# Twelve tiles of v under the inverse of the small blocks, four in the scan, and the adaptive sums ordered behind the masks of the scan preparation

## The chip, the cores and the metric

The kernel runs on one core of a Trainium2 chip. The metric is the device time of one execution in microseconds (us). The engines are TensorE (PE, matrix products; its weight loads are listed apart as PEld), VectorE (DVE), ScalarE (ACT), GpSimd (POOL) and SyncE (SP, which issues most transfers).

## The reference, cut to what matters

The program is a trunk of two layers for one sequence of 256 tokens and 2048 channels, in float32. Layer 0 mixes tokens with an RWKV-7 time mix, layer 1 with a convolution module; each is followed by a gated channel mixer (FFN). Before each of the four sub-layers the input is normalised and modulated by shift, scale and gate vectors made from a conditioning vector c; these vectors are the matrix-vector products called adaptive sums here. What the change touches is the time mix of layer 0:

```python
mod = silu(c) @ ada_w[i] + ada_b[i]            # the adaptive sums: 6 vectors of 2048 a layer
sh_m, sc_m, g_m, sh_f, sc_f, g_f = split(mod, 6)
r, k, v = einsum('nbtc,ncd->nbtd', x_rkv, w_rkv)
def step(S, inp):                              # one token, a 64 x 64 state for each of 32 heads
    sa = einsum('bhij,bhj->bhi', S, a_t)
    S = S * w_t + sa[..., None] * b_t + v_t[..., None] * k_t
    return S, einsum('bhij,bhj->bhi', S, r_t)
y = group_norm(scan(step, S0, (r, decay, k, v, -kk, kk * a)))
out = ((y + bonus) * g) @ w_o
x = x + g_m * out
h = modulate(rms_norm(x), sh_f, sc_f);  x = x + g_f * conv_glu_ffn(h)
```

## The kernel before, in words

Channels lie on the 128 partitions in 16 tiles (KT), each with two heads; tokens lie along the free axis. Products whose weights are streamed from DRAM come in two kinds. A split product rounds the weight to a short-mantissa part `hi` (ScalarE, L232) and a rest `lo` (VectorE or GpSimd, L233) and runs three matmuls for each of 16 pieces (L243 to L245, 48 a tile). A native product (`linear_native`, L306) runs one fp32 matmul a piece on the raw weight and needs no other engine.

The scan is not done token by token. The 256 tokens are cut into four chunks of 64 (NC_ = 4), and within a chunk the dependence is a triangular system, whose inverse is built from blocks of 32. VectorE inverts all the small blocks at once (`inv_step`, L592 to L599, helper lines L151 and L157), in two halves; the result X goes to DRAM (dT and dTn, L642 and L646) and is read back in another layout for each channel tile (`prep_load2`, L676 and L677). While VectorE inverts, PE makes the first V0 = 8 of 16 tiles of v by `v_tile`, with native products.

Then comes the scan stage, L652 to L887. For each channel tile f there is

- `prep_gen`: products of keys and queries (L704, called twice), a transpose (L712) copied by ScalarE (L713), two masks on VectorE (L710 for `strict`; L716, `gr`, for `incl`, both recorded at helper line L157), the completion of the inverse (L724, L749, copied by VectorE at L752), the centred v (L740) and a bonus (L755);
- `chain_gen`: four dependent chunks, each with L769, a copy on ScalarE (L774), L782, a copy on ScalarE (L784), L788 and the state update on VectorE (L793 or helper L160 called from L791);
- `gn_gen`: the group normalisation, for tiles 0 to 3, 4 to 7, 8 to 11, 12 and 13, 14 and 15 together (L805 to L831);
- and, as filler between these, `v_gen` (the other eight tiles of v, as split products) and `wo_gen` (the first NWO tiles of the output projection, half of their rows).

A heap written by hand sets the order of PE in this stage: each generator yields a planned delay, `at(t, ...)` puts it in at a planner time, PD = 13 units are one channel tile's period, and PE takes its instructions in the order in which the heap emits them (`manual_schedule`). The v_gen of the i-th split tile starts at (V1 + i VP) PD, here 13 i. The other engines' instructions, and SP's transfers, are ordered by the framework's scheduler, which simulates the program and gives each engine the instruction that is ready first; the order is then fixed, and each engine works through its own in turn.

The adaptive sums of later pieces have no close user. `ada` loads 1 MB of weights (L206) and makes one vector piece on VectorE with two multiply-and-sum instructions of 1024 columns (L209; the profile prints CUSTOM_DVE_ANT_0, the order ISA; each is followed by a short read of the accumulator). `bg_gen` emits one sum at planner time 0 and then one each 10 units (BGT, L859; each 7 units, BGT2, from the sum BGN on). Sums without a release condition may be put by the scheduler anywhere on VectorE's order where their weights are there.

Of the kernel before, what the change touches and what calls it, by code (L numbers as in the profile page):

```python
# [14 lines left out]
ALU = mybir.AluOpType  # L15
# [3 lines left out]
P = 128  # L19
# [7 lines left out]
L = 64  # L27
NC_ = T // L
# [3 lines left out]
GN_EPS = 64e-5  # L32
NS = 44
NT = 26
V0 = 8
RP = 1
PL = 10
PUP = 1.05
# [10 lines left out]
BG_G = 2  # L49
BGT = 10.0  # L50
VS = 0.42
V1 = 0.0
VP = 1.0
KM = 10
TPE = (1,)*14+(3,14)
TPO = (2,)*14+(4,5)
# [56 lines left out]
def trunk_kernel(ctx: ExitStack, tc: tile.TileContext, a, out):  # L113
    nc = tc.nc
# [17 lines left out]
    def slot512():  # L132
        return slot().rearrange("p a t -> p (a t)")[:, :2 * T]
# [22 lines left out]
    def vmul(o, x, y):  # L156
        nc.vector.tensor_tensor(out=o, in0=x, in1=y, op=ALU.mult)  # L157

    def stt(o, x, s, y, op0=ALU.mult, op1=ALU.add):
        nc.vector.scalar_tensor_tensor(out=o, in0=x, scalar=s, in1=y, op0=op0, op1=op1)  # L160
# [11 lines left out]
    def K(n):  # L172
        o, w = COFF[n]
        return cst[:, o:o + w]
# [6 lines left out]
    incl = K("incl").rearrange("p (c t) -> p c t", c=2)  # L181
# [10 lines left out]
    def mod(l, piece, f):  # L192
        return md[l][:, piece * KT + f:piece * KT + f + 1]
# [7 lines left out]
    def ada(l, piece, f, r=None):  # L201
        parts = 4 if r else TQ if l == 0 and piece != 5 else 2
        w = C // parts
        if r is None:
            r = raw_tile()
            nc.sync.dma_start(out=r, in_=a["ada"][l, piece, f])  # L206
            r = [r[:, q * w:(q + 1) * w] for q in range(parts)]
        for q in range(parts):
            nc.vector.tensor_tensor_reduce(  # L209
                out=r[q], in0=r[q], in1=cb[:, q * w:(q + 1) * w], scale=1.0,  # L210
                scalar=mod(l, piece, f) if q else pc("ada_b", (l * 6 + piece) * KT + f),
                op0=ALU.mult, op1=ALU.add, accum_out=mod(l, piece, f))
        if piece in (1, 4):
            g = "gam_mix" if piece == 1 else "gam_ffn"
            j = 0 if piece == 1 else KT
            stt(geff[l][:, j + f:j + f + 1], mod(l, piece, f), 1.0, pc(g, l * KT + f), ALU.add, ALU.mult)
# [3 lines left out]
    def bg(n):  # L220
        for _ in range(min(n, len(jobs))):
            ada(*jobs.pop(0))
# [44 lines left out]
    def linear(src, ops, tag=None, cols=T, eng=None, step=1024):  # L267
        return linears([src], ops, tag, cols, eng, None, step)[0]
# [45 lines left out]
    def split_x(src, o):  # L314
        nc.scalar.copy(o[:, 0, :T], src)  # L315
        vsub(o[:, 1, :T], src, o[:, 0, :T])
# [207 lines left out]
    def r_more(n):  # L524
        for _ in range(n):
            if rnext[0] < KT:
                for q in range(RP):
                    r_load(rnext[0] + q)
                r_tile(rnext[0])
                rnext[0] += 1  # L530
# [55 lines left out]
    def v_tile(f):  # L586
        acc = linear_native(vraw.pop(f) if f in vraw else load_w(a["w_rkv"][2, f]), xv32, ("c", "y")[f % 2])
        vt[f] = t1()
        nc.scalar.copy(vt[f], acc[:, :T])
# [34 lines left out]
    for s in range(1, 31):  # L624
# [3 lines left out]
        if s % NF == 1:  # L628
            if rnext[0] < KT:
                r_more(1)  # L630
            elif len(vt) < V0:
                v_tile(len(vt))
    r_more(KT)
    xv = []
    for f in range(KT):
        xv.append(slot(F32R))
        split_x(xv32[f], xv[f])
    while len(vt) < V0:
        v_tile(len(vt))
# [17 lines left out]
    def v_gen(f):  # L657
        acc = ps("mm")
        r = load_w(a["w_rkv"][2, f])
        yield 0  # L660
        for k0 in range(0, KT, 8):
            hi, lo = split_w(r, k0, k0 + 8, 512, VE[0])
            for k in range(k0, k0 + 8):
                mm_pair(acc, hi, lo, k - k0, xv[k], k == 0, k == KT - 1)
                yield VS
        vt[f] = t1()
        nc.scalar.copy(vt[f], acc[:, :T])
# [18 lines left out]
    def prep_gen(f):  # L686
        ari, bk, tt, tn = ld.pop(f)
        v = vt.pop(f)
        gr = slot512().rearrange("p (c h t) -> p c h t", c=NC_, h=2)
# [7 lines left out]
        def bank(mm):  # L697
            pg = ps("g")
            for c in range(NC_):
                mm(pg[:, c * P:(c + 1) * P], bk[:, c].rearrange("p j t -> p (j t)"), c)  # L700
            return pg.rearrange("p (c h t) -> p c h t", c=NC_, h=2)

        def times(j):
            return bank(lambda o, b, c: nc.tensor.matmul(o, lhsT=b, rhs=ari[j][:, c].rearrange("p h t -> p (h t)"), start=True, stop=True, skip_group_check=True))  # L704

        pg = times(0)
# [5 lines left out]
        pg = bank(lambda o, b, c: nc.tensor.transpose(out=o, in_=b, identity=ident))  # L712
        nc.scalar.copy(tk, pg.rearrange("p c h t -> p c (h t)"))  # L713
        yield PU
        pg = times(1)
        vmul(gr, pg, incl.unsqueeze(1).to_broadcast([P, NC_, 2, L]))  # L716
        yield 2.4

        py = ps("g")
# [116 lines left out]
    def xview(f):  # L836
        return xs[f // 2][:, f % 2, :T]

    def x_load(f):
        if xs[f // 2] is None:  # L840
            xs[f // 2] = slot()
            nc.sync.dma_start(out=xs[f // 2][:, :, :T], in_=a["xT"][:, f - f % 2:f - f % 2 + 2, :])


    def wo_gen(m):
        x_load(m)
        r = load_w(a["w_o"][m][:, :C // 2])
        yield 0
        acc = ps("mm")
        hi, lo = split_w(r, 0, KT // 2, 512, VE[0])  # L850
        for k in range(KT // 2):
            mm_pair(acc, hi, lo, k, yo[k], k == 0, k == KT // 2 - 1)
            yield VS
        stt(xview(m), acc[:, :T], mod(0, 2, m), xview(m))

    def bg_gen(n):
        for i in range(n):
            bg(1)
            yield BGT if i < BGN else BGT2  # L859

    heap, seq = [], [0]
# [1 line left out]
    def at(t, g):  # L863
        heapq.heappush(heap, (t, seq[0], g))
        seq[0] += 1

    for f in range(KT):
        at((f - 1) * PD, load_gen(f))
        at(f * PD, prep_gen(f))
        at((f + 1) * PD + 0.3, ("chain", f))  # L870
    for i, f in enumerate(range(V0, KT)):
        at((V1 + i * VP) * PD, v_gen(f))
    for fs in ((0, 1, 2, 3), (4, 5, 6, 7), (8, 9, 10, 11), (12, 13), (14, 15)):
        at((fs[-1] + 3) * PD + 3.0, gn_gen(fs))
    jobs[:0] = [(0, 2, f) for f in range(NWO)]
    jobs += [(0, 2, f) for f in range(NWO, NG)]
    at(0, bg_gen(99))
    for m in range(NWO):
        at(WO0 * PD + m * WOP, wo_gen(m))
    with tc.manual_schedule(engines={mybir.EngineType.PE}):  # L880
# [229 lines left out]
    with tc.manual_schedule(engines=CME):  # L1110
        for f in range(KT):
            e0, e1 = (nc.gpsimd if i >= LOV else nc.vector for i in (2 * f, 2 * f + 1))
            pg = linear(a["w_pw1"][KT + f], ops, "g", T + 2, e0, LST)
# [11 lines left out]
        with tc.manual_schedule(engines=TME):  # L1125
# [30 lines left out]
            for f in range(max(KT + 4, AST + NAQ)):  # L1156
# [11 lines left out]
                if 0 <= g < KT:  # L1168
                    (nc.gpsimd if g % XP == XP - 1 else nc.vector).tensor_tensor(
                        out=cops[g][:, 1, :T], in0=tv[g], in1=cops[g][:, 0, :T], op=ALU.subtract)  # L1170
# [130 lines left out]
```

## Time and profile before

| what | value |
|---|---|
| time, median of 3 runs | 2644.01 us (2635.43 to 2644.99) |
| the profiled execution | 2645.53 us |
| its span, first to last instruction | 2643.8 us |
| granted TensorE clock, mean | 0.974 |
| PE, DVE, ACT, POOL busy | 94%, 77%, 51%, 19% |
| DMA over the span | 237 GB/s read and written |

The times come from runs without a profile; the trace and all its rows come from one execution with a profile, so that its own time is the one that a sum of rows is held against. A busy share is a mean over all stages: the stage of this change lies between 350 and 800 us, in which PE's share by slices falls below its mean. The clock is given as a share of the full 2.4 GHz; 0.5 is the lower level, 1.2 GHz. Matmuls are pipelined, so that the busy time of a group of them is told better by the starts of the group and of the next than by the sum of their durations. In a row of the timeline the numbers are the start, the time from the first to the last end of the instructions merged in it, the engine, the line, the operation, output and inputs with their shapes, the count, and in brackets the idle time before it and what ended that.

### The profile page before, as it was taken

How to read it: one execution, taken by the hardware profiler on the slowest of the kernel's cores; microseconds unless marked ns; L12 is line 12 of the kernel's file. 1: busy time of each engine (PE TensorE's matmuls, PEld its weight loads, DVE VectorE, ACT ScalarE, POOL GpSimd, SP SyncE). 2: the span in 40 equal slices, each digit the busy share in tenths (PEclk: the TensorE clock that was granted, in tenths of full speed). 3: DMA queues.
4: the chain of work that ended last, by engine and by line, in shares of the span. 5: the costliest groups of instructions: out<-in, count | busy, mean ns of one | idle time of the engine just before them, and what ended most of it. 6: DMA issues, size and time to landing. Idle time of an engine off the chain costs nothing.

```text
span 2643.8 us, 45213 instructions
## 1 busy us (share of the span) xinstructions
PE 2487.3 (94%) x17330; PEld 2198.6 (83%) x17330; DVE 2032.6 (77%) x3611; ACT 1354.6 (51%) x2548; POOL 499.4 (19%) x492
## 2 busy tenths in 40 slices
PE   5899997998999999999999989988899999999997
PEld 3688886877798888888888779987888888888886
DVE  5567766667578889888888989989998866666666
ACT  4566623565556543554455455554575445534554
POOL 0000015454002012002100248964320000000000
PEclk9999998998899999999999999989999999999999
DMA  8887767777275779878977854445667755555553
GB/s 322 323 316 275 205 204 237 236 220 239 89 274 209 286 281 338 303 288 303 332 286 281 294 205 147 173 144 225 269 237 284 279 188 190 183 184 194 188 182 121
DMA packets 169624, 630.35 MB, mean 238 GB/s; under 512 B 77376, under 2 KB 89152, under 8 KB 110784
## 3 DMA queue, kind: packets, MB, share of 16 engines
q1 hardware_dynamic: 168672, 624.85, 66.7%
q8 instruction: 136, 2.23, 0.3%
q0 software_dynamic: 736, 2.62, 0.3%
q14 instruction: 80, 0.66, 0.1%
HBM read 614.30 MB, written 13.11 MB: 237 GB/s over the span
## 4 chain that ended last, share of the span: by engine, by line
PE 73%; DVE 13%; DMA 7%; ACT 3%; issue 3%; SPq 1%; POOL 1%; DVEq 0%; ACTq 0%; POOLq 0%
PE ps L240 29%; PE ps L241 15%; PE ps L243 6%; PE ps L245 6%; PE ps L244 6%; DMA raw<-ada 3%; DVE raw L209 3%; DVE lo L233 3%; DVE s L160 3%; PE ps L378 1%; ACT hi L232 1%; PE ps L704 1%; DMA raw<-w_dn 1%; ACT t L163 1%; DVE s L154 1%
## 5 line engine op out<-in xcount | busy, mean ns | idle before, releaser
L240 PE MATMUL ps<-s,hi 128*128 128x512 f32 x3872 | 1361.2, 396 | 1.0 <-DVE s L154 0.7
L232 ACT CAST hi<-raw 128x1024 fp32r<-128x1024 f32 (+6 forms) x873 | 768.5, 897 | 902.9 <-PE ps L240 463.0
L241 PE MATMUL ps<-s,lo 128*128 128x256 f32 x3872 | 1086.3, 281 | 8.6 <-DVE lo L233 8.5
L233 DVE TENSOR_TENSOR lo<-raw,hi 128x1024 fp32r<-128x1024 f32 (+4 forms) x639 | 750.4, 1177 | 315.8 <-ACT hi L232 313.8
L240 PEld LDWEIGHTS ps<-s,hi 128*128 128x128 f32 x3872 | 727.2, 188 | 171.7 <-DVE s L154 1.0
L241 PEld LDWEIGHTS ps<-s,lo 128*128 128x128 f32 x3872 | 732.4, 189 | 15.2 <-DVE lo L233 13.7
L243 PE MATMUL ps<-s,hi 128*128 128x256 f32 (+1 forms) x1712 | 503.0, 295 | 7.7 <-ACT hi L232 6.3
L245 PE MATMUL ps<-s,lo 128*128 128x256 f32 (+1 forms) x1712 | 490.3, 287 | 18.7 <-DVE lo L233 18.6
L233 POOL TENSOR_TENSOR lo<-raw,hi 128x512 fp32r<-128x512 f32 x234 | 334.6, 1455 | 823.7 <-ACT hi L232 779.1
L244 PE MATMUL ps<-s,hi 128*128 128x256 f32 (+1 forms) x1712 | 489.9, 286 | 0.0
L245 PEld LDWEIGHTS ps<-s,lo 128*128 128x128 f32 x1712 | 330.4, 193 | 26.1 <-DVE lo L233 21.3
L243 PEld LDWEIGHTS ps<-s,hi 128*128 128x128 f32 x1712 | 330.3, 193 | 16.4 <-ACT hi L232 8.5
L244 PEld LDWEIGHTS ps<-s,hi 128*128 128x128 f32 x1712 | 331.3, 194 | 4.2 <-issue 3.3
L209 DVE CUSTOM_DVE_ANT_0 raw<-raw,cb,par 128x1024 f32<-128x1024 f32 x156 | 211.3, 1354 | 75.2 <-DMA raw<-ada 71.3
L209 DVE CUSTOM_DVE_ANT_0 raw<-raw,cb,md 128x1024 f32<-128x1024 f32 x156 | 215.6, 1382 | 1.0
L160 DVE SCALAR_TENSOR_TENSOR s<-ps,par,s 128x239 f32<-128x239 f32 (+26 forms) x412 | 163.0, 455 | 1.8 <-ACT s L163 1.2
L1200 POOL TENSOR_TENSOR s<-s,t 128x256 f32<-128x256 f32 x6 | 4.1, 728 | 704.0 <-DVE t L333 704.0
L160 DVE SCALAR_TENSOR_TENSOR s<-ps,md,s 128x256 f32<-128x256 f32 x213 | 100.7, 480 | 26.6 <-PE ps L241 20.2
L160 DVE SCALAR_TENSOR_TENSOR t<-t,par,t 128x255 f32<-128x255 f32 (+1 forms) x172 | 84.4, 491 | 1.1
L163 ACT ACTIVATE t<-t,par 128x256 f32<-128x256 f32 x118 | 67.8, 584 | 11.4 <-DVE t L157 9.5
L315 ACT CAST s<-t 128x256 fp32r<-128x256 f32 x150 | 59.0, 402 | 19.7 <-DVE t L157 17.0
L154 DVE TENSOR_TENSOR s<-t,s 128x256 fp32r<-128x256 f32 x150 | 67.9, 462 | 1.4
(208 smaller groups left out, 2356.3 us busy)
## 6 DMA issues: line engine op xcount, KB each, us to landing
raw<-w_up SPq DMA_DIRECT2D x172, 1024.0 KB, 4.9
raw<-ada SPq DMA_DIRECT2D x156, 1024.0 KB, 6.5
raw<-w_dn SPq DMA_DIRECT2D x64, 896.0 KB, 4.6
raw<-w_pw SPq DMA_DIRECT2D x48, 1024.0 KB, 4.8
raw<-w_rkv SPq DMA_DIRECT2D x38, 1024.0 KB, 6.0
raw<-ada_s SPq DMA_DIRECT2D x32, 1024.0 KB, 6.7
raw<-w_dn SPq DMA_DIRECT2D x32, 960.0 KB, 6.3
raw<-w_o SPq DMA_DIRECT2D x11, 1024.0 KB, 5.8
```

The costliest lines, as they stand in the source:

```text
L154: nc.vector.tensor_tensor(out=o, in0=x, in1=y, op=ALU.subtract)
L160: nc.vector.scalar_tensor_tensor(out=o, in0=x, scalar=s, in1=y, op0=op0, op1=op1)
L163: nc.scalar.activation(out=o, in_=i, func=func, bias=bias, scale=scale)
L209: nc.vector.tensor_tensor_reduce(out=r[q], in0=r[q], in1=cb[:, q * w:(q + 1) * w], scale=1.0, scalar=mod(l, piece, f) if q else pc("ada_b" ...
L232: nc.scalar.copy(hi[:, s], v[:, s])
L233: (eng or nc.vector).tensor_tensor(out=lo[:, s], in0=v[:, s], in1=hi[:, s], op=ALU.subtract)
L240: nc.tensor.matmul(acc.rearrange("p (a t) -> p a t", a=2), lhsT=hi[:, c], rhs=x[:, :, :T], start=first, stop=False, skip_group_check=True)
L241: nc.tensor.matmul(acc[:, T:], lhsT=lo[:, c], rhs=x[:, 0, :T], start=False, stop=last, skip_group_check=True)
L243: nc.tensor.matmul(acc[:, :n], lhsT=hi[:, c], rhs=x[:, 0, :n], start=first, stop=False)
L244: nc.tensor.matmul(acc[:, :n], lhsT=hi[:, c], rhs=x[:, 1, :n], start=False, stop=False)
L245: nc.tensor.matmul(acc[:, :n], lhsT=lo[:, c], rhs=x[:, 0, :n], start=False, stop=last)
L315: nc.scalar.copy(o[:, 0, :T], src)
```

## The change

V0 goes from 8 to 12: four more tiles of v are made by native products right behind the first eight, before the scan's own work on PE. The four that are left to `v_gen` start at planner times 13, 44.2, 75.4 and 106.6 (V1 = 1.0, VP = 2.4). The `incl` mask of each preparation, the same multiplication as before, is now issued directly, and its instruction kept in `last[0]`; each sum that `bg_gen` emits is issued under `tc.issue_after(last[0])`, which lets the scheduler put its VectorE instructions, and its load, no earlier on their engines than after that mask. `bg_gen` starts at planner time 3.0, behind the first preparation's mask.

```diff
-V0 = 8
+V0 = 12
-V1 = 0.0
-VP = 1.0
+V1 = 1.0
+VP = 2.4
...
         pg = times(1)
-        vmul(gr, pg, incl.unsqueeze(1).to_broadcast([P, NC_, 2, L]))
+        last[0] = nc.vector.tensor_tensor(out=gr, in0=pg, in1=incl.unsqueeze(1).to_broadcast([P, NC_, 2, L]), op=ALU.mult).ins
         yield 2.4
...
+    last = [None]
...
     def bg_gen(n):
         for i in range(n):
-            bg(1)
+            with tc.issue_after(last[0]):
+                bg(1)
             yield BGT if i < BGN else BGT2
...
-    at(0, bg_gen(99))
+    at(3.0, bg_gen(99))
```

The first place is PE's order behind the tiles of v, up to the first chain step (L769). In the kernel before, raw_4273 is the weight tile of the eighth native tile, and L243 to L245 on hi_4391 are the first split tile, which stands between the steps of the first preparation:

```order
L306 MATMUL ps_4275<-s_1688,raw_4273 128x256 x2
L704 MATMUL ps_4383<-s_3972,s_4097 128x128 x4
L243 MATMUL ps_4376<-s_4298,hi_4391 128x256
L244 MATMUL ps_4376<-s_4298,hi_4391 128x256
L245 MATMUL ps_4376<-s_4298,lo_4392 128x256
...
L712 MATMUL ps_4409<-cst,s_4097 128x128 x4
```

In the changed kernel raw_4409 is the weight tile of the twelfth native tile, and the preparation stands alone behind it:

```order
L306 MATMUL ps_4411<-s_1688,raw_4409 128x256 x2
L704 MATMUL ps_4460<-s_3972,s_4097 128x128 x4
L712 MATMUL ps_4468<-cst,s_4097 128x128 x4
L704 MATMUL ps_4474<-s_3973,s_4097 128x128 x4
L724 MATMUL ps_4484<-tn_4442,n_761_4452 32x32 x8
L740 MATMUL ps_4501<-cst,t_4021 64x64 x8
L749 MATMUL ps_4512<-s_3968,ys_4485 32x32 x8
L755 MATMUL ps_4523<-t_4496,cst 128x256
L704 MATMUL ps_4553<-s_3974,s_4142 128x128 x4
L243 MATMUL ps_4546<-s_4298,hi_4561 128x256
```

Every step of the first preparation, the one that reads the inverse (L724, on tn_4442) too, now comes behind all twelve native tiles and ahead of the first split tile. On SP's queue the load of the eleventh native tile (tile 10) stands behind the first reads of the inverse (L676 and L677 for f = 0), which wait for the store of dT; the load of the twelfth takes the buffer of X, and so waits for the stores that read it.

The second place is VectorE at the end of the small-block inverse (raw_3963 is one half of X, s_3966 and s_3967 its products, L641 the diagonal, md_72 the vectors of the sums):

```order
 L157 TENSOR_TENSOR s_3967<-raw_3963 128x84
 L641 MEMSET raw_3963 128x32
 L151 TENSOR_TENSOR raw_3963<-raw_3963,s_3967 128x28x3
-L209 ISA raw_4379,md_72<-raw_4379,cb,par 128x1024
-L209 ISA md_72 128x1
 L157 TENSOR_TENSOR s_3967<-raw_3963 128x58
-L209 ISA raw_4379,md_72<-raw_4379,cb,md_72 128x1024
-L209 ISA md_72 128x1
```

The sums between the last steps of the inverse are gone from there.

The third place is VectorE from the sixteenth, last `incl` mask on. In the kernel before (L157 with cst is that mask, on 128x512) the last chains and normalisations follow, and no sum:

```order
L157 TENSOR_TENSOR s_7462<-ps_7525,cst 128x512
L831 TENSOR_TENSOR s_7522<-t_7278,s_7522 128x256
L752 COPY s_3971<-ps_7589 32x4x32 x2
L157 TENSOR_TENSOR t_7608<-ps_7606,t_6015 128x256
L160 SCALAR_TENSOR_TENSOR s_7253<-ps_7492,plc,Sp_7572 64x64 x2
```

In the changed kernel the mask is recorded at L716, and sums follow it at once (one sum is two instructions on raw_..., each with its short read on md_72):

```order
L716 TENSOR_TENSOR s_7286<-ps_7344,cst 128x512
L209 ISA raw_7350,md_72<-raw_7350,cb,par 128x1024
L209 ISA md_72 128x1
L209 ISA raw_7430,md_72<-raw_7430,cb,par 128x1024
L209 ISA md_72 128x1
...
L831 TENSOR_TENSOR s_7341<-t_7097,s_7341 128x256
L752 COPY s_3971<-ps_7409 32x4x32 x2
L209 ISA raw_7350,md_72<-raw_7350,cb,md_72 128x1024
L209 ISA md_72 128x1
```

Of the 34 sums of this stage (68 instructions of 1024 columns), all stand ahead of that mask in the order before; in the order of the changed kernel 42 instructions stand ahead of it and 26 behind it.

## Rows read from the trace of the kernel before

**Rows 1.** Timeline of PE, 350 to 445 us: start, us, engine, line.

```profile
358.77 49.82 PE L306 MATMUL ps<-s,raw 128*128 128x256 f32 x228
...
408.43 1.05 PE L704 MATMUL ps<-s,s 128*128 128x128 f32 x8
...
410.73 0.60 PE L712 MATMUL ps<-cst,s 128*128 128x128 f32 x4
...
428.08 0.71 PE L724 MATMUL ps<-tn,n 32*32 32x32 f32 x16 [12.68 <-DMA tn<-dTn]
...
430.94 1.28 PE L740 MATMUL ps<-cst,t 128*64 128x64 f32 x16
...
436.62 0.76 PE L749 MATMUL ps<-s,ys 32*32 32x32 f32 x16 [4.40 <-DMA s<-dT]
437.31 1.22 PE L755 MATMUL ps<-t,cst 128*128 128x256 f32 x2
438.32 1.92 PE L704 MATMUL ps<-s,s 128*128 128x128 f32 x8
...
440.81 0.48 PE L769 MATMUL ps<-s,s 64*64 64x64 f32 x4
```

**Rows 2.** Windows: stretch, its us, busy by engine (instructions), clock, DMA share, GB/s.

```profile
408.60:440.80 32.20, 15.12 (x129) 14.00 (x128) 18.04 (x37) 8.46 (x19) 16.10 (x16) 0.70 0.66 200
440.80:682.00 241.20, 220.30 (x2482) 186.55 (x2482) 167.46 (x341) 135.24 (x420) 107.42 (x109) 0.90 0.72 231
682.00:713.80 31.80, 27.04 (x241) 20.77 (x238) 14.94 (x34) 15.01 (x52) 0.00 (x0) 0.95 0.03 10
740.00:760.00 20.00, 20.00 (x172) 20.00 (x171) 17.67 (x31) 10.49 (x19) 0.00 (x0) 1.00 0.78 286
```

**Rows 3.** The chain that ended last, in order of time, 405 to 425 us.

```profile
412.16 6.77 DMA dT<-raw
```

**Rows 4.** The page's DMA issues: count, KB each, median us to landing.

```profile
raw<-w_rkv SPq DMA_DIRECT2D x38, 1024.0 KB, 6.0
```

**Rows 5.** Timeline of VectorE, 635 to 641 us.

```profile
636.63 1.28 DVE L209 CUSTOM_DVE_ANT_0 raw<-raw,cb,par 128x1024 f32<-128x1024 f32 x1
```

**Rows 6.** Timeline of GpSimd, 380 to 411 us.

```profile
400.39 10.21 POOL L233 TENSOR_TENSOR lo<-raw,hi 128x512 fp32r<-128x512 f32 x4 [33.60 <-ACT hi L232]
```

**Rows 7.** Timeline of VectorE, 404 to 421 us.

```profile
404.64 0.50 DVE L151 TENSOR_TENSOR raw<-raw,s 128x108 f32<-128x108 f32 x2
405.06 1.53 DVE L157 TENSOR_TENSOR s<-raw 128x84 f32<-128x84 f32 x2
...
406.52 1.31 DVE L151 TENSOR_TENSOR raw<-raw,s 128x84 f32<-128x84 f32 x1
...
409.35 1.41 DVE L151 TENSOR_TENSOR raw<-raw,s 128x150 f32<-128x150 f32 x1
```

**Rows 8.** Windows of preparations, columns as in rows 2.

```profile
443.40:458.30 14.90, 13.25 (x160) 11.74 (x159) 11.05 (x21) 7.81 (x23) 10.49 (x6) 1.00 0.97 351
522.60:544.60 22.00, 21.34 (x222) 17.67 (x221) 14.91 (x29) 15.46 (x44) 16.53 (x17) 1.00 0.82 276
557.50:566.70 9.20, 8.64 (x134) 7.17 (x134) 4.02 (x12) 6.57 (x26) 2.48 (x5) 1.00 0.80 233
566.70:580.30 13.60, 11.39 (x136) 9.70 (x137) 9.83 (x22) 5.94 (x24) 0.93 (x3) 0.75 0.67 204
580.30:605.70 25.40, 23.00 (x185) 16.72 (x185) 19.77 (x38) 13.12 (x41) 11.61 (x14) 0.73 0.68 216
647.20:677.30 30.10, 24.68 (x173) 18.38 (x171) 18.13 (x35) 15.37 (x41) 2.84 (x3) 0.61 0.56 183
```

**Rows 9.** Waits of PE, 440 to 720 us: total, times, longest.

```profile
PE ps L769 <- DVE s L160: 9.9, 10, 2.8
PE ps L769 <- DVE s L793: 6.0, 7, 2.1
```

**Rows 10.** Timeline of VectorE, 713 to 720 us.

```profile
715.01 3.49 DVE L233 TENSOR_TENSOR lo<-raw,hi 128x1024 fp32r<-128x1024 f32 x3
```

## The prediction

> **What bounds the kernel now.** I read the page's engine shares first, then the stretch table of the time from the small-block inverse to the output projection, then TensorE's (PE's) and VectorE's (DVE's) instructions in order of time at its seams, then who waits for whom. The profiled execution took 2645.53 us (its span is 2643.8); the median of the runs shown is 2644.01, 1.5 lower. The sum is made against 2645.5, and 1.5 is taken off at the end.
>
> The change lives between 350 and 714 us. It has three parts with three limits. Up to 408.6 PE makes eight tiles of v with native fp32 matmuls while VectorE inverts the small blocks: 49.82 us for 228 records of 32 a tile, 7.0 us a tile [rows 1]. From 408.6 to 440.8 PE is busy for 15 of 32 us, at a mean granted clock of 0.70 [rows 2]: the inverse is written to DRAM and read back, and PE stands for 12.7 us before L724 and 4.4 before L749 [rows 1]. Then the scan: to 682 PE is busy for 220 of 241 us at 0.90, VectorE for 167 [rows 2]. Last a tail of 31.8 us, from the sixteenth `incl` mask to the first residual add of the output projection, in which VectorE works for 14.9 us and the DMA share is 0.03 [rows 2]: the last two chains are short of everything but latency.
>
> **The change, part by part.** *Four more native tiles.* PE goes on for 4 x 7.0 = 28.0 us after 408.6 and ends at 436.6, in the hole that the round trip leaves. Before its first chain step (L769) there then come L704, L712, L704, L724, L740, L749, L755, L704. With the durations shown (the first L704 counts twice) that is 8.6 us [rows 1]; the five from L724 on, 5.9 us of it, ran where the clock was mostly at the lower of its two levels (1.2 and 2.4 GHz), and at the upper they would take about half, so 5.6 to 8.6. L769 starts at 442.2 to 445.2, against 440.81: +1.4 to +4.4. What hides the tiles is the round trip; if their weights are late the cover is gone. The load of tile 10 stands on SP's queue behind the first reads of the inverse (L676), which wait for its store: issued at 412.16, 6.8 us, over at 418.95 [rows 3]. A load that starts there and takes the 6.0 us of the page's w_rkv loads [rows 4] is there at 425, and PE wants it at 422.6: 2.4 us, and more if the clock falls in the gap. I take +3 for the start of the scan, range +1 to +9.
>
> *The inverse's end.* Two adaptive sums (four instructions of 1.28 us [rows 5]) leave the end of the inverse's second half, and GpSimd's (POOL's) split for the first v tile leaves its first: while GpSimd ran four of these, 400.4 to 410.6, four VectorE instructions (three are shown) took 1.3 to 1.5 us, where pairs took 0.5 [rows 6, 7]. About 1 us each, 4 us, so the store could leave at 408, the load of tile 10 start at 415 and land at 421, in time. The Trainium skill ("SBUF — State Buffer", section "SBUF: two separate sides") says that VectorE with two SBUF inputs and GpSimd exclude each other for whole instructions; by that these 4 us come back, and without it nothing does and tile 10 is 2.4 us late. The trace agrees at this place, and the range holds both. Since PE is busy to 436.6 either way, I count no further gain.
>
> *Four fewer split tiles in the scan.* One has 48 matmuls; with 172 in 20 full us [rows 2] that is 0.116 each, 5.6 us. Of the eight, the first ran in the hole, so 7 fall to 4 behind the chains' start: 3 x 5.6 = 16.8 us at most. From one preparation's transpose copy (L713) to the next took 14.9 us with a split tile, 9.2 and 13.6 without [rows 8]: the last two show 1.3 to 5.7 a tile, 4 to 17 in all. I take 5 each, -15, nearer to the row where PE is never out of work.
>
> *The sums behind the masks.* A sum is two VectorE instructions, and 34 sums are left at this point. In the order of before all 68 instructions stand ahead of the sixteenth mask, and none behind it. In the new order 42 stand ahead and 26 behind, since the 13 sums that the planner emits after it may no longer rise above it. This has two sides. Ahead of it VectorE loses 26 x 1.28 = 33.3 us of work. PE's waits for VectorE's state updates were 9.9 and 6.0 us [rows 9], 16 in all, and GpSimd's splits fall too; bounds 0 and -16, I take half, -8. Behind it the tail must hold these 33.3 us, its own 14.9 [rows 2] and the first three splits of the output weights, 3.5 us [rows 10], which stood earlier before: 51.7 us if VectorE never waits, 19.9 more than 31.8. If nothing of it fits beside the old tail it is 36.8 more. The sums stand between the chains' updates in the order, so most fill what was idle (16.9 us of the 31.8); their 1 MB loads have no other traffic there. I take +23. Three output tiles' matmuls, part of which PE did early before, wait for the same end and cost nothing beyond it.
>
> Sum: +3 - 15 - 8 + 23 = +3; 2645.5 + 3 - 1.5 = 2647. A change of under 0.5% (13.2 us) is about what a measurement of this kernel cannot tell from none.
>
> **The rivals.** *The clock falls in the thinner scan (slower).* Split tiles were what PE did while the chains waited. The stretch that holds the first group normalisation took 22.0 us at clock 1.00 with a split tile beside it; the second and third took 25.4 at 0.73 and 30.1 at 0.61 without a v tile [rows 8]. Two of the five preparations that lose their tile, and the first normalisation, can go the way of the 13.6 us row (0.75) and the 25.4 us row. Price: the gain on the tiles shrinks from 15 to 4, and the first normalisation costs 25.4 where 22.0 less 5.6 was hoped for, +9, less 3 of this that the sum already has: +17, 2664. It decides where PE stands still for some 2 us before a chain step in a stretch without a split tile. The Trainium skill ("TensorE: Matmul & The Clock Gate", section "HAM oscillation — how this bites in real kernels") warns of gaps between bursts of matmuls that bring the lower clock back; the rows agree. Against it: 9.2 us at 1.00, with no filler at all.
>
> *The sums don't fit beside the chains (slower).* If a chain update waits behind two or three sums every time, the tail grows by 36.8, not 23: +14, 2661. For it: each update is behind PE and ScalarE in turn. Against it: 16.9 us idle.
>
> *The scan is freed more than I think (faster).* The second normalisation stretch (580.3 to 605.7) holds 8 sum instructions in the order of before and 4 now. If it then stays at the upper clock, it takes what the first would without its tile, 22.0 - 5.6 = 16.4, not 25.4: -9. If PE's waits for the updates go whole, that is -16, not -8: -8. And if VectorE never waits in the tail, that costs 19.9, not 23: -3. All three make -20, 2627. For it: both waits are for VectorE, and it is what the sums were queued on. Against it: each of the three is the best end of its bounds.
>
> **How the numbers follow.** The forecast, about as before, has 0.52; the clock rival 0.18, the tail rival 0.10, the faster one 0.20. The forecast's own range, from its bounds near the values taken, is 2637 to 2657. To leave out no more than 2 in 10 the range goes to 2627 and 2664. Faster by over 0.5% (under 2630.8): 0.19, most of the faster case and a little of the forecast's edge; slower (over 2657.2): 0.27, the two slow cases nearly whole; within: 0.54.
>
> **What would show it.** Right: L306 runs without a gap to about 437; L769 first at 442 to 445; the sixteenth mask some 20 us earlier than 682; behind it 26 sum instructions with VectorE busy almost throughout, and the first residual add 50 to 58 us after the mask. Wrong: a gap in L306 near 422 with the clock at half behind it (late weights); a mask later than 672 with stretches below clock 0.8 (the clock rival); more than 60 us from the mask to the residual add (the tail rival); a mask before 650 (the faster one). The forecast fails if the tail and the scan do not pay each other off within 13 us.

## The result, and the profile after

The changed kernel took 2665.76 us (median of 4, 2651.77 to 2677.89) against 2643.64: a ratio of 1.0089, interval 1.0063 to 1.0115. It is slower by 0.9%, 1.8 us outside the range of the prediction. The profiled execution is the fastest of the four, 2651.77 us with a span of 2650.0, so its trace understates the loss; the first experiment gives a second one.

The windows of the changed kernel (stretch, its us, busy by engine, clock, DMA share, GB/s) from the last native matmul to the first chain step, from there to the sixteenth `incl` mask, and to the third residual add:

```profile
439.50:445.50 6.00, 5.89 (x81) 5.11 (x80) 4.14 (x8) 4.64 (x12) 4.33 (x5) 1.00 0.50 169
445.50:670.30 224.80, 201.73 (x2330) 167.16 (x2330) 131.35 (x295) 125.05 (x406) 79.09 (x100) 0.89 0.57 176
670.30:726.70 56.40, 40.88 (x253) 29.69 (x252) 51.40 (x95) 20.28 (x56) 0.00 (x0) 0.61 0.70 256
```

Against [rows 2] the scan is 16 us shorter, and the tail, 32.6 us to the same third add, is 56. In it VectorE is busy for 51.4 us of 56.4; the prediction had 51.7 of work there. PE, at a granted clock of 0.61, was busy for 40.9 us with 253 matmuls, and waited for VectorE besides. Its timeline at the native tiles answers [rows 1]:

```profile
362.02 77.46 PE L306 MATMUL ps<-s,raw 128*128 128x256 f32 x356
439.32 1.05 PE L704 MATMUL ps<-s,s 128*128 128x128 f32 x8
...
441.77 0.44 PE L724 MATMUL ps<-tn,n 32*32 32x32 f32 x16
...
443.15 0.44 PE L749 MATMUL ps<-s,ys 32*32 32x32 f32 x16
...
445.50 0.33 PE L769 MATMUL ps<-s,s 64*64 64x64 f32 x4
```

The tiles run without a gap, and L724 and L749, which waited for 12.7 and 4.4 us, wait for nothing. In the window of [rows 9], 440 to 720 us, PE's waits for the state updates grew from 15.9 to 27.0 us, where the forecast let them fall by half. That window holds the scan and a part of the tail. In the scan alone, from the first chain step to the sixteenth mask, they were in the kernel before

```profile
PE ps L769 <- DVE s L160: 8.5, 8, 2.8
PE ps L769 <- DVE s L793: 4.8, 6, 2.1
```

and in the changed kernel

```profile
PE ps L769 <- DVE s L160: 8.9, 9, 1.8
PE ps L769 <- DVE s L793: 8.0, 10, 1.7
```

So the scan's part grew from 13.3 to 16.9 us, and the rest of the growth lies in the tail. The start of the tail on VectorE, and what PE waits for in it:

```profile
670.25 0.69 DVE L716 TENSOR_TENSOR s<-ps,cst 128x512 f32<-128x512 f32 x1
670.86 1.28 DVE L209 CUSTOM_DVE_ANT_0 raw<-raw,cb,par 128x1024 f32<-128x1024 f32 x1
...
676.62 1.28 DVE L209 CUSTOM_DVE_ANT_0 raw<-raw,cb,md 128x1024 f32<-128x1024 f32 x1
...
678.28 0.57 DVE L160 SCALAR_TENSOR_TENSOR s<-ps,plc,Sp 64x64 f32<-64x64 f32 x2
```

```profile
678.91 0.48 PE L769 MATMUL ps<-s,s 128*64 128x64 f32 x4 [5.73 <-DVE s L160]
```

Four sum instructions of 1.28 us follow the mask at once, a fifth after two short steps, and the state update that the chain needs comes only at 678.28; PE stands for 5.73 us.

For the comparisons below each trace is cut at four starts: the first native matmul of v (L306), the first chain step (L769), the sixteenth `incl` mask and the third residual add. "Before a" is the trace shown ahead of the prediction. Ratios are to runs of the kernel before on the same chip.

| kernel | ratio (interval) | start | scan | tail | sums in the tail |
|---|---|---|---|---|---|
| before a | | 90.7 | 241.2 | 32.6 | 0 |
| before b (base) | | 89.8 | 235.7 | 31.1 | 0 |
| changed a | 1.0089 (1.0063 to 1.0115) | 92.1 | 224.7 | 56.5 | 26 |
| changed b (again) | 1.0093 (1.0067 to 1.0119) | 96.4 | 232.7 | 56.4 | 26 |
| tiles | 1.0048 (1.0030 to 1.0066) | 104.4 | 228.9 | 33.8 | 0 |
| sums | 1.0072 (1.0044 to 1.0099) | 80.5 | 231.9 | 55.4 | 26 |
| pace | 1.0107 (1.0080 to 1.0135) | 98.2 | 257.7 | 35.0 | 0 |
| late20 | 1.0079 (1.0058 to 1.0100) | 91.6 | 237.1 | 55.4 | 26 |
| first8 | 0.9989 (0.9974 to 1.0004) | 81.8 | 246.1 | 31.0 | 0 |
| first10 | 1.0000 (0.9977 to 1.0024) | 89.8 | 239.0 | 34.6 | 0 |
| first12 | 1.0011 (0.9994 to 1.0028) | 93.0 | 236.9 | 31.0 | 0 |
| v14 | 1.0108 (1.0082 to 1.0134) | 105.8 | 221.3 | 57.0 | 26 |
| mid8 | 1.0071 (1.0044 to 1.0097) | 80.3 | 249.2 | 42.7 | 12 |
| mid10 | 1.0074 (1.0047 to 1.0101) | 89.7 | 240.4 | 42.7 | 12 |
| upd12 | 0.9968 (0.9949 to 0.9988) | 98.5 | 216.0 | 32.5 | 0 |
| upd10 | 0.9983 (0.9962 to 1.0004) | 90.8 | 233.0 | 32.5 | 0 |
| upd8 | 1.0012 (0.9990 to 1.0035) | 79.1 | 243.8 | 31.7 | 0 |

"Sums in the tail" counts instructions of 1024 columns (L209) that ran there. One trace is one execution: two of the same kernel differ by 5.5 and 8.0 us in the scan, so differences of that size in single traces decide nothing by themselves.

### The profile page after: what moved, and what is told of

Read it like the earlier page. It is cut to its first block, busy times and chain, and to the rows that moved or that the text cites. A ratio compares the mean times of both kernels' runs of the same rounds, so it can differ in the third digit from the quotient of the medians.

```text
span 2650.0 us, 45060 instructions
## 1 busy us (share of the span) xinstructions
PE 2499.1 (94%) x17266; PEld 2204.4 (83%) x17266; DVE 2019.8 (76%) x3611; ACT 1345.8 (51%) x2532; POOL 454.6 (17%) x476
## 4 chain that ended last, share of the span: by engine, by line
PE 77%; DVE 12%; DMA 5%; ACT 3%; issue 2%; POOL 1%; SPq 0%; DVEq 0%; ACTq 0%; POOLq 0%
PE ps L240 31%; PE ps L241 16%; PE ps L243 6%; PE ps L245 6%; PE ps L244 6%; DVE raw L209 4%; PE ps L306 3%; DVE s L160 2%; DVE lo L233 2%; DMA raw<-ada 2%; DMA raw<-ada_s 1%; PE ps L704 1%; PE ps L378 1%; ACT t L163 1%; ACT hi L232 1%
## 5 line engine op out<-in xcount | busy, mean ns | idle before, releaser
L232 ACT CAST hi<-raw 128x1024 fp32r<-128x1024 f32 (+5 forms) x857 | 759.9, 902 | 878.0 <-PE ps L240 452.9
L240 PEld LDWEIGHTS ps<-s,hi 128*128 128x128 f32 x3872 | 727.0, 188 | 169.0
L241 PEld LDWEIGHTS ps<-s,lo 128*128 128x128 f32 x3872 | 731.6, 189 | 16.0 <-DVE lo L233 14.4
L243 PE MATMUL ps<-s,hi 128*128 128x256 f32 (+1 forms) x1648 | 481.9, 293 | 7.7 <-ACT hi L232 7.3
L245 PE MATMUL ps<-s,lo 128*128 128x256 f32 (+1 forms) x1648 | 473.0, 288 | 17.0 <-DVE lo L233 17.0
L244 PE MATMUL ps<-s,hi 128*128 128x256 f32 (+1 forms) x1648 | 471.4, 286 | 0.0
L233 POOL TENSOR_TENSOR lo<-raw,hi 128x512 fp32r<-128x512 f32 x218 | 301.7, 1409 | 790.9 <-ACT hi L232 591.9
L245 PEld LDWEIGHTS ps<-s,lo 128*128 128x128 f32 x1648 | 318.5, 194 | 24.1 <-DVE lo L233 19.5
L243 PEld LDWEIGHTS ps<-s,hi 128*128 128x128 f32 x1648 | 318.5, 193 | 16.0 <-ACT hi L232 10.2
L244 PEld LDWEIGHTS ps<-s,hi 128*128 128x128 f32 x1648 | 319.7, 194 | 3.7 <-issue 3.0
L209 DVE CUSTOM_DVE_ANT_0 raw<-raw,cb,par 128x1024 f32<-128x1024 f32 x156 | 206.3, 1326 | 53.0 <-DMA raw<-ada 52.2
L209 DVE CUSTOM_DVE_ANT_0 raw<-raw,cb,md 128x1024 f32<-128x1024 f32 x156 | 210.3, 1352 | 1.0
L160 DVE SCALAR_TENSOR_TENSOR s<-ps,par,s 128x239 f32<-128x239 f32 (+26 forms) x412 | 163.0, 456 | 1.9 <-ACT s L163 1.3
L160 DVE SCALAR_TENSOR_TENSOR s<-ps,md,s 128x256 f32<-128x256 f32 x213 | 100.9, 480 | 29.0 <-PE ps L241 21.5
L160 DVE SCALAR_TENSOR_TENSOR t<-t,par,t 128x255 f32<-128x255 f32 (+1 forms) x172 | 85.3, 496 | 1.1
L306 PE MATMUL ps<-s,raw 128*128 128x256 f32 x384 | 83.8, 380 | 0.1
L306 PEld LDWEIGHTS ps<-s,raw 128*128 128x128 f32 x384 | 72.6, 190 | 10.6 <-issue 0.8
```

The source lines that it names most:

```text
L209: nc.vector.tensor_tensor_reduce(out=r[q], in0=r[q], in1=cb[:, q * w:(q + 1) * w], scale=1.0, scalar=mod(l, piece, f) if q else pc("ada_b" ...
L232: nc.scalar.copy(hi[:, s], v[:, s])
L233: (eng or nc.vector).tensor_tensor(out=lo[:, s], in0=v[:, s], in1=hi[:, s], op=ALU.subtract)
L240: nc.tensor.matmul(acc.rearrange("p (a t) -> p a t", a=2), lhsT=hi[:, c], rhs=x[:, :, :T], start=first, stop=False, skip_group_check=True)
L241: nc.tensor.matmul(acc[:, T:], lhsT=lo[:, c], rhs=x[:, 0, :T], start=False, stop=last, skip_group_check=True)
L243: nc.tensor.matmul(acc[:, :n], lhsT=hi[:, c], rhs=x[:, 0, :n], start=first, stop=False)
```

## The experiments

**The change again, and its two halves.** The first has no edit. The second moves only the tiles, the third only the sums (V0 8, V1 0.0, VP 1.0):

```diff
# tiles
-            with tc.issue_after(last[0]):
-                bg(1)
+            bg(1)
...
-    at(3.0, bg_gen(99))
+    at(0, bg_gen(99))
# sums
-V0 = 12
+V0 = 8
```

> The changed kernel unchanged, for more of its times and a second trace. In its first trace the stage cost +7 us (scan start +1.5 when the head's own +3.2 is taken off, scan -16.4, tail +22.5) and its time was the lowest of four, 2651.8; the others lie 10 to 26 us above. Theory A (the tail behind the sixteenth mask is bound by VectorE's 26 sum instructions): the median stays at 2655 to 2668 and the tail from that mask to the third residual add takes 52 to 56 us in this trace too. Theory B (the scan with fewer split tiles loses TensorE's clock, and how much differs from run to run): the scan from the first chain step to the sixteenth mask, 225 us in the first trace, takes 235 us or more when the time is over 2660.

> Only the tiles of v move (V0 12, V1 1.0, VP 2.4); the sums are issued as before, at planner time 0 and free of the masks; 2 of their 70 instructions stand behind the sixteenth mask. Theory A: the tail is 32 to 36 us as before, the scan keeps its gain of about 16, so 2626 to 2634. Theory B: the thinner scan itself is what costs, so 2650 to 2665, with the scan at 235 us or more.

> Only the sums move (behind the masks, from planner time 3.0); eight native tiles and eight split tiles as before; 26 sum instructions stand behind the sixteenth mask. Theory A: the tail grows by about 22 us and the scan gives back at most 8, so 2655 to 2668. Theory B: the scan is as full as before and keeps its clock, so 2640 to 2650.

Measured: 2664.17, 2652.59 and 2658.81 us, where the kernel before had 2638.14. The tail belongs to the sums alone: 55.4 with them, 33.8 without. The rest of theory A fell: the tiles alone cost 0.5% and gain nothing. Their trace shows why in part; the start is 104.4, because sums that are free to rise stand ahead of the first masks on VectorE and wait there for their loads, and L749 behind these:

```profile
455.44 0.63 PE L749 MATMUL ps<-s,ys 32*32 32x32 f32 x16 [4.89 <-DVE s L157]
```

The sums alone give the start 10 us back. Some 5 of these are the inverse's second half, which is no longer interrupted: counted from the first native matmul its store is issued at 64.3 us, where it was 69.1 before. In the second trace of the change the start is late for another reason:

```profile
451.18 1.22 PE L755 MATMUL ps<-t,cst 128*128 128x256 f32 x2 [3.04 <-POOL t L732]
```

GpSimd's multiplication for the bonus (L732) stood behind the split of the first split tile, whose weights came late. The scan is 232.7 at 0.86, and the time of this execution some 19 us above the first trace's: head +5, start +4, scan +8, the rest +2.

**No sum in the tail by pace.**

```diff
-BGT = 10.0
+BGT = 5.7
-BGT2 = 7
+BGT2 = 5.7
```

> The changed kernel with the sums emitted every 5.7 planner units (10 and then 7 before), so that all 34 come before the sixteenth mask, two or three instruction pairs to a preparation, and none stands behind it. Theory A: the tail falls back to 32 to 36 us and the scan takes the 33 us of VectorE's work again, in part beside PE: 2628 to 2640. Theory B: the scan is as thin as in the changed kernel and has more sums in it, so 2655 to 2670.

Measured: 2669.28 us. The tail is 35.0, as theory A wants, but the scan took 257.7, 25 more than in the changed kernel's longer trace:

```profile
455.90:713.60 257.70, 223.31 (x2327) 184.94 (x2326) 163.45 (x345) 128.80 (x406) 78.43 (x98) 0.80 0.64 204
```

PE's waits for the state updates in it:

```profile
PE ps L769 <- DVE s L160: 12.6, 10, 1.8
PE ps L769 <- DVE s L793: 11.6, 9, 2.4
```

So the tail is not the whole cause; the sums cost as much in the scan. One preparation on VectorE, and PE's chain steps behind it:

```profile
594.79 0.69 DVE L716 TENSOR_TENSOR s<-ps,cst 128x512 f32<-128x512 f32 x1 [0.83 <-PE ps L704]
595.40 1.28 DVE L209 CUSTOM_DVE_ANT_0 raw<-raw,cb,par 128x1024 f32<-128x1024 f32 x1
596.60 0.08 DVE L209 DVE_READ_ACCUMULATOR2_ANT md<- 128x1 f32 x1
596.60 0.58 DVE L793 TENSOR_SCALAR s<-ps,plc 64x64 f32<-64x64 f32 x2
597.21 1.28 DVE L209 CUSTOM_DVE_ANT_0 raw<-raw,cb,par 128x1024 f32<-128x1024 f32 x1
598.42 0.08 DVE L209 DVE_READ_ACCUMULATOR2_ANT md<- 128x1 f32 x1
598.53 0.58 DVE L160 SCALAR_TENSOR_TENSOR s<-ps,plc,Sp 64x64 f32<-64x64 f32 x2
```

```profile
597.23 0.34 PE L769 MATMUL ps<-s,s 128*64 128x64 f32 x4 [1.49 <-DVE s L793]
599.17 0.48 PE L769 MATMUL ps<-s,s 128*64 128x64 f32 x4 [1.49 <-DVE s L160]
```

Mask, sum, update, sum, update: each update waits out a sum, and PE each update. This made a third theory: it is the place behind the mask, and so ahead of the next state updates, that costs.

**The first split tile later; sums bound to the first mask alone; the kernel before again.** (first8 and first10 differ from first12 in V0, V1 and VP: 8, 0.0, 1.0 and 10, 0.6, 1.5.)

```diff
# late20
-V1 = 1.0
+V1 = 2.0
# first12
-        last[0] = nc.vector.tensor_tensor(out=gr, ...).ins
+        g_ = nc.vector.tensor_tensor(out=gr, ...).ins
+        last[0] = last[0] or g_
```

> The kernel before, unchanged, for a second trace on the chip of the other runs. In the first trace the first native matmul of v starts at 350.1 us, in five traces of other kernels with the same order up to there at 353 to 358. If the head's 3 to 8 us are the chip's state, this trace starts at 350 to 358 too; if they come from the change, at 350 again. From the first native matmul to the first chain step 88 to 95 us, the scan 235 to 245, the tail 31 to 34.

> The changed kernel with the first split tile a preparation later (V1 2.0 for 1.0), so that GpSimd's first multiplication for the bonus (L732) stands ahead of the split of that tile's weights and not behind it. Theory A (the start of the scan hangs on that load, through GpSimd's order, 92 to 96 us from the first native matmul to the first chain step; the tail of 56 us is the sums'): the start falls to 90 to 93 with no wait of L755 for GpSimd, the tail stays 54 to 58, the time falls by 2 to 6 to 2658 to 2664. Theory B (the start was late because the clock or the head was): it stays at 92 to 97 and the time at 2664 or over.

> The tiles as in the kernel before (eight native, eight split); the sums start at planner time 3.0 and may not stand ahead of the first preparation's incl mask, but are free of all later ones; none stands behind the sixteenth. Theory A (what the sums cost is the tail, and what their delay gives is the end of the inverse, which came 10 us earlier in the kernel with only the sums moved): start about 80, scan 235 to 242 with the sums' waits for their loads as before, tail 32 to 34; together 8 to 14 less than before, 2625 to 2633 where before has 2638. Theory B (sums cost wherever they stand in the scan): 2636 to 2645.

> The changed kernel with its sums free of all masks but the first: twelve native tiles, four split ones, 2 sum instructions behind the sixteenth mask. Theory A: start 92 to 97, scan 225 to 232, tail 33 to 35, together 5 to 12 less than before, so 2626 to 2635. Theory B (with twelve native tiles the scan has too little work for TensorE between the chains and loses its clock): scan 235 or more, 2645 or more.

> Ten native and six split tiles, sums free of all masks but the first, none of them behind the sixteenth. Theory A: a start of 80 to 86 as the native tiles stay inside the round trip, a scan between those of eight (246) and twelve (237) native tiles, 236 to 242, a tail of 30 to 33: 2628 to 2638, under the kernel before. Theory B (the start hangs on other loads, as with twelve tiles): a start of 90 or more, 2638 to 2648.

Measured: 2638.23 (one run), 2658.99, 2637.99, 2644.52 and 2640.21 us. late20 starts at 91.6 with no wait of L755, as theory A had it; its time moved little (1.0079 for 1.0089 and 1.0093). With the sums free of the later masks the loss is gone with eight, ten and twelve native tiles (0.9989, 1.0000, 1.0011). But none of the three gains, as theory A would have it: their scans, 246.1, 239.0 and 236.9, are about as long as before's or longer. And ten tiles are not hidden by the round trip, though that was expected: over all runs but before and tiles the start is 79 to 82 with eight, some 90 with ten, 92 to 99 with twelve. The second trace of before gives the head 351.7, among 349.7 to 360.2 of all; up to there PE and VectorE have the same order in all of them, so this spread is not the change's.

**Fourteen native tiles; half of the sums in the tail.** v14 has V0 14 and VP 4.8; mid8 and mid10 have BGT 8.0, BGT2 6.0 and the tiles of first8 and first10.

```diff
# v14
-V0 = 12
+V0 = 14
-VP = 2.4
+VP = 4.8
# mid8, mid10
-BGT = 10.0
+BGT = 8.0
-BGT2 = 7
+BGT2 = 6.0
```

> The changed kernel with fourteen native tiles and two split ones (V0 14, VP 4.8; sums behind every mask as in the change). Theory A (a split tile is worth 5 us of TensorE's time in the scan, as the prediction had it): the scan falls by 8 to 12 from the 225 and 233 of the changed kernel, to 214 to 224. Theory B (the scan's length is set by the chains' own round trips through ScalarE and VectorE and by the clock, and the split tiles only fill): it stays at 224 to 238, while the start grows by two native tiles, 14 us, to 105 to 112; the time is then 2672 to 2682. The tail is 54 to 58 by both.

> Eight native and eight split tiles as before, sums behind the masks as in the change but emitted each 8 and then 6 planner units, so that 12 sum instructions (15.4 us of VectorE) stand behind the sixteenth mask instead of 26. Theory A (VectorE's work is what the tail lasts): 14.9 + 3.5 + 15.4 = 33.8 us of work in a tail of 31 us, so a tail of 36 to 42, a start of 80 to 82, a scan of 232 to 240; 2636 to 2648. Theory B (any sum behind the mask delays the chains): a tail over 45.

> As the run with 12 sum instructions behind the sixteenth mask, but with ten native tiles and six split ones (V0 10, V1 0.6, VP 1.5). The ten native tiles end some 14 us after eight, still inside the round trip of the inverse. Theory A: a start of 80 to 86, a scan of 228 to 236, a tail of 36 to 42; 2634 to 2646. Theory B (each split tile taken from the scan costs its clock): a scan over 240.

Measured: 2670.5, 2663.61 and 2662.0 us. v14's scan is 221.3, between the two theories (7 below the mean of the changed kernel's two, 3.7 a tile) and not apart from either by more than traces differ. The tail follows the number of sums: 0, 12 and 26 of them make 31 to 35, 42.7 and 55 to 57 us, some 0.9 us each. But mid8's scan is 249.2, with 14 more sum instructions in it than the run sums with its 231.9, and its time (1.0071) is no better than that of sums (1.0072), with 26 in the tail: what leaves the tail is paid again in the scan.

**The sums behind the updates.** The tiles and pace of the pace run, with `last[0]` taken from the chain's updates instead of the mask; upd8 and upd10 have the tiles of first8 and first10.

```diff
# against pace
-        last[0] = nc.vector.tensor_tensor(out=gr, ...).ins
+        g_ = nc.vector.tensor_tensor(out=gr, ...).ins
+        last[0] = last[0] or g_
...
-                        stt(uv[hr, c + 1, h, :], pch[hr, wc], plc[hr, f, c:c + 1], Sp[hr, h, :])
+                        last[0] = nc.vector.scalar_tensor_tensor(out=uv[hr, c + 1, h, :], ...).ins
...
-                        nc.vector.tensor_scalar(out=uv[hr, 1, h, :], ...)
+                        last[0] = nc.vector.tensor_scalar(out=uv[hr, 1, h, :], ...).ins
```

> The paced kernel (twelve native tiles, a sum each 5.7 planner units, none behind the sixteenth mask) with one difference: each sum is ordered behind the latest state update of a chain emitted so far and not behind the latest mask. In VectorE's order 26 of 41 groups of sums of the paced kernel stand directly ahead of an instruction of L160 or L793 (the state updates and residual adds); here it is 8 of 42. Theory A (sums that stand ahead of the updates hold the chains up): the scan falls from 258 to 228 to 240 us, the time from 2669 to 2638 to 2652. Theory B (so many sums in the scan, or any ordering of them, cost this): the scan stays at 250 or more and the time at 2660 or more.

> The same order behind the updates with eight native and eight split tiles. Theory A: the start at 80 to 84 as in the other kernels whose sums stay out of the inverse's end, a scan of 235 to 245, a tail of 30 to 35: 2628 to 2642. Theory B: a scan of 255 or more, 2650 or more.

> The same order behind the updates with ten native and six split tiles. Theory A: a start of 82 to 90, a scan of 232 to 242, a tail of 30 to 35: 2626 to 2642. Theory B: a scan of 250 or more, 2650 or more.

Measured: 2632.23, 2643.10 and 2637.51 us beside 2639.52; upd8 lies 1 us above what was expected. The one edit between pace and upd12 is the sums' place, with 63 sum instructions in the scan of each. PE's order is nearly the same in both; the scheduler also moved some of the other engines' instructions. The scan fell from 257.7 to 216.0, further than expected. Of the 42 us, 14 are idle time of PE (34.4 to 20.5), nearly all of it waits for the updates (24.2 to 10.8), and 28 are busy time for about as many matmuls (223.3 to 195.4), at a granted clock that rose from 0.80 to 0.93. Both follow from the edit; that the waits bring the clock down was not tried by itself. Its window, its waits of PE there, and a preparation on VectorE (lines one further on: L792 and L794 are the updates):

```profile
455.10:671.00 215.90, 195.43 (x2338) 163.55 (x2338) 174.00 (x345) 126.97 (x408) 93.73 (x99) 0.93 0.76 243
```

```profile
PE ps L770 <- DVE s L794: 6.7, 8, 1.7
PE ps L770 <- DVE s L792: 4.1, 8, 1.8
```

```profile
570.71 0.69 DVE L716 TENSOR_TENSOR s<-ps,cst 128x512 f32<-128x512 f32 x1
571.31 0.57 DVE L794 TENSOR_SCALAR s<-ps,plc 64x64 f32<-64x64 f32 x2
571.92 0.58 DVE L792 SCALAR_TENSOR_TENSOR s<-ps,plc,Sp 64x64 f32<-64x64 f32 x2
572.53 1.29 DVE L209 CUSTOM_DVE_ANT_0 raw<-raw,cb,par 128x1024 f32<-128x1024 f32 x1
...
573.86 1.28 DVE L209 CUSTOM_DVE_ANT_0 raw<-raw,cb,md 128x1024 f32<-128x1024 f32 x1
...
575.19 0.58 DVE L753 COPY s<-ps 32x128 f32<-32x128 f32 x2
```

Mask and updates now come first, and the sums fill the time until the chains' next step. (The counts of groups in the expectation take in L160 instructions that belong to the sums themselves, one column of `geff<-md,par`; ahead of a state update stand 17 groups of sums in pace's scan and 1 in upd12's.) Added up over the 86 half updates that ran in each scan, the time from the end of the last L788 matmul to the update's start in which VectorE ran sums is 41.8 and 42.3 us in before (62 sums in the scan), 58.8 in both traces of the change (40 and 38 sums), 70.3 in sums (38), 97.5 in pace (63) and 17.9 in upd12 (63). With tiles, pace and number of sums held, the place decides: this bears out the third theory. Across kernels with other tiles or fewer sums the figure does not order the scans (sums has 70.3 and a scan of 231.9). upd12 is faster than both kernels: 0.9968 of before (0.9949 to 0.9988).

## Why the prediction was wrong

**The start was right.** The twelve tiles run through, tile 10's weights were there, and the start grew by 1.4 to 6.6 us over the four pairs of traces, mean 4.0; the forecast had 3, range 1 to 9. The stores of the inverse were issued at 408.1 and 410.2 with the head's 3.25 us taken off. The forecast had 408, by the 4 us that VectorE was to get back with GpSimd's split gone; GpSimd is idle there now, and in the row of [rows 7] where 84 columns took 1.53 us the pair takes 0.51:

```profile
408.10 0.54 DVE L151 TENSOR_TENSOR raw<-raw,s 128x108 f32<-128x108 f32 x2
408.52 0.51 DVE L157 TENSOR_TENSOR s<-raw 128x84 f32<-128x84 f32 x2
```

By the Trainium skill ("SBUF — State Buffer", section "SBUF: two separate sides") that is what the exclusive pair of ports would do, and the trace agrees here; in the run sums, where GpSimd's split still runs at that place, the pair takes 1.54 us.

**The tail was right.** +23 was forecast, +23.9 and +25.3 is what the two pairs show, and the terms of it too: 51.7 us of work forecast, 51.4 busy.

**The scan was wrong, and with it the sum.** The failed step is "PE's waits for VectorE's state updates were 9.9 and 6.0 us, 16 in all [...] bounds 0 and -16, I take half, -8". It let the waits fall with the number of sums ahead of the mask, and its 16 took in 2.6 us of the tail. Fewer sums are left there, 42 of 68 instructions, but the waits did not fall: in the scan they are 13.3 and 13.1 us in the two traces of before, 16.9 and 16.6 in the change's, and 13.9 in sums, which moves the sums alone. What counts is the instruction that a sum stands ahead of. In VectorE's order in the scan 8 of 51 groups of sums stand directly ahead of a state update before, 13 of 31 in the change, 17 of 39 in pace with its 24.2 us of waits, and 1 of 40 in upd12 with 10.8. A bound that allowed no loss was wrong: the order of the changed kernel showed the new places, and only the count was read from it.

Of -15 for the tiles and -8 for the sums, -23, the scan gave 9.7 (means of two traces each). PE's idle time in it grew by 2.0 us, from 20.9 and 21.5 to 23.1 and 23.3, where the sums were to take 8 away; its busy time fell by 11.7 where the tiles were to take 15. So 10 of the 13 us that are missing stand in the term for the sums. The sixteenth mask, forecast some 20 us earlier than 682, came 12 earlier and in the second trace 5 later, with the head's 3 and 8 us in it.

The term for the tiles by itself is less certain. In each of three pairs the scan loses the matmuls of three split tiles (2482 records against 2338), 16.8 us at the prediction's price, and gets shorter by 9.1 us (first8 to first12), 9.5 (the mean of before to tiles) and 27.8 (upd8 to upd12, where the updates are kept clear). These are single traces, and -15 lies among them.

The stages' sum over the means of two traces is +4.0 - 9.7 + 24.6 = +18.9 against the +3 forecast, 13 of the 16 in the scan; the head, +4.9, and the rest of the program, -4.4, nearly cancel. The time's own +22 to +26 is near that.

**The rivals.** The clock rival had the time, 2664, but not the cause: the larger part of what was missing is idle time. The stretch that it named did go the way it said, though not as far: the first normalisation now has the lower clock for part of it, 23.5 us for 22.0. The second takes 31.0 for 25.4, with more matmuls in it (238 for 185), and the third has left the lower clock, 19.1 for 30.1 in [rows 8].

```profile
518.30:541.80 23.50, 20.09 (x166) 14.93 (x168) 9.98 (x21) 14.55 (x45) 13.78 (x18) 0.71 0.56 180
578.30:609.30 31.00, 27.44 (x238) 20.36 (x237) 14.18 (x30) 18.09 (x54) 18.99 (x23) 0.67 0.51 162
647.70:666.80 19.10, 17.35 (x172) 12.82 (x172) 13.11 (x30) 11.95 (x37) 2.31 (x3) 0.91 0.51 189
```

Over the scan the clock is 0.89 and 0.86 against 0.90 and 0.92, so that a share of the 3.3 us by which PE's busy time fell too little can be the clock's. But upd12, as thin in tiles, has 0.93: few split tiles alone do not bring it down. Between pace and upd12 it goes with PE's waits, 0.80 with 24.2 us of them and 0.93 with 10.8. The Trainium skill's warning of gaps between bursts of matmuls ("TensorE: Matmul & The Clock Gate", section "HAM oscillation — how this bites in real kernels") speaks of waits for DMA; the trace of pace agrees that the clock is lower where the gaps are more, but here the gaps came from VectorE's order and not from missing filler. The tail rival (36.8) did not come, nor did the faster one.

Open: why the rest of the program behind the third add is some 4 us shorter in the changed kernel's traces than in before's, how much of the scan's loss the clock would have cost without the waits, and what the head's spread comes from.

## What to carry to other kernels

An engine with idle time left can still set the time, by what stands ahead of a short urgent instruction in its fixed order: look at which instruction each piece of filler precedes, not at the engine's share or the number of pieces. Order filler behind the latest urgent instruction (here the chain's state update), not behind an event that an urgent instruction follows. Filler that has a last place to be, here the gates of the residual add, must be paced so that none is left when the cover runs out: behind it each sum instruction cost the tail some 0.9 of the 1.28 us that it takes.

## What the runs showed of the hardware

The stores of the inverse landed in 3.1 us at the median in the changed kernel and in 7.5 before, though the DMA engines moved as much in that stretch (405 to 445 us, 227 and 194 GB/s). It goes with the tiles and not with the sums: 3.1 in first10, tiles, pace and upd12, with ten or twelve native tiles, and 8.1 to 8.2 in first8, upd8 and sums, with eight. Which of the loads beside them makes the difference was not tried. And PE's busy time is no measure of its work: the tail's 243 matmuls took 26.0 us of busy time at a clock of 1.00 (before b), 253 took 40.9 at 0.61 (the change).
